# Attention products of 64 and 16 contraction rows are issued as products of all 128 rows, padded with zeros

## The chip, the cores and the metric

The kernel runs on one core of a Trainium2 chip. TensorE (PE) multiplies: a weight load puts the stationary operand into the array (one row per partition that is summed over, up to 128 rows and 128 columns), and a matmul streams the moving operand past it. VectorE (DVE), ScalarE (ACT) and GpSimd (POOL) do the elementwise work, SyncE (SP) issues the DMAs. The metric is the time of one execution in microseconds. The kernel before takes 2603.17 us, the median of three runs between 2599.4 and 2603.88 us.

## The reference, cut to what matters

Two transformer blocks run one after the other on 16 meta tokens and 512 real ones (L = 528 rows, width 1024). The first has two layers, with three kinds of attention over both blocks:

```
layer A: stick-breaking attention, 16 heads of 64: z = q k^T / 8,
         w = exp(log_sigmoid(z) + sum over later keys of log_sigmoid(-z)), o = w v
layer B: differential attention, 8 heads: o = (softmax(q1 k1^T / 8) - lam softmax(q2 k2^T / 8)) v,
         q1, q2, k1, k2 of 64 dims, v of 128
mixer:   forgetting attention, 8 heads of 64: softmax(q k^T / 8 + c_t - c_s) v,
         and a gated linear recurrence, 8 heads of 128 (chunks; the first one is the 16 meta rows)
each of A and B is followed by an MLP, the mixer by a mixture of 32 experts, 2 per token
```

All of it is float32. A float32 number x is split into a high part that the array multiplies in one pass (fp32r) and the rest x - high, and a product is high x high plus the two cross terms.

## The kernel before

TensorE's instructions stand in the order in which the program writes them; the instructions of the other engines are ordered by a scheduler from that and from priorities. Attention is a generator of steps that is interleaved with dense products (projections of the next heads, split weights taken one tile ahead by `take`, L135), by estimated times in layer A (`pace`, L230) and by fixed counts of dense steps in layer B and the mixer (`script`, L753).

Scores. The 64 dims of two heads lie on partitions 0 to 63 and 64 to 127 of one tile. `stack` (L330) makes for each head s a key operand of 128 rows: high parts in the head's own 64 rows, low parts in the other 64. `double` (L338) makes for the queries: out[s] with the high parts in all rows, and out[2] with the low parts of both heads, each in its own rows. So the scores of a region are two accumulating products, one of 128 rows (high q against high and low k) and one of 64 rows (low q against high k):

```
ops = [(zr, kz[s][:, ks], qz[s][:, a:b]), (zr, kz[s][r, ks], qz[2][r, a:b])]      # sb_qk, L475
ops = [(zr, q[s][:, qs], k[s][:, a:b]), (zr, q[2][r, qs], k[s][r, a:b])]          # scores, L787
```

In layer A a pair of heads has four units (`SB_UNITS`) with regions of 272, 144 and 16, of 400, of 272 and of 256 columns; in layer B and the mixer a pair has four query tiles with 144, 272, 400 and twice 264 key columns. A third product (identity against a mask) follows on the diagonal, and in the mixer one with the forget gates. In all there are 216 products of 64 rows: 96 in layer A (recorded at L481), 80 in layer B and 40 in the mixer (both at L793).

Values. 528 keys are four tiles of 128 and one of 16 rows: `natural` (L444) transposes v into vn[:, 0..3, :] and vn[:16, 4, :], `flip` (L822) does the same for the weights, wT. The product with v has a part of 16 rows: in layer A at L525 (`pv`), in layer B at L901 (512 columns, first of five parts), in the mixer at L1160, and in the recurrence at L1260 (kn[:16, 3, :] against vn[:16, 4, :]). These operands are plain float32, for which a matmul stands in the trace as two records. Where two heads share a bank (L525, L1160), their outputs take 64 columns of the array each.

POOL multiplies the weights of layer B by the norm's gains (L132) and does one multiplication of each rotation (L689). It works its instructions off in order.

Of the kernel before, what the change touches and what calls it, by code (L numbers as in the profile page):

```python
# [7 lines left out]
F32 = mybir.dt.float32  # L8
# [10 lines left out]
NM = 16  # L19
S = 512  # L20
# [9 lines left out]
class Net:  # L30
# [43 lines left out]
    # ---- weights: loaded some tiles ahead, split one tile ahead of their use  # L74
# [60 lines left out]
    def take(self):  # L135
        """the next weights (hi, lo)"""
        nc = self.nc
        while len(self.splitq) < 2 and self.rawq and not self.rawq[0][1]:
            raw, _ = self.rawq.pop(0)
            kt = raw.shape[1]  # L140
            hi = self.wsp.tile([128, KT, 128], F32R, name="whi")[:, :kt, :]
            lo = self.wsp.tile([128, KT, 128], F32R, name="wlo")[:, :kt, :]
            with self.tc.high_priority(offset=self.AHEAD_W):
                nc.scalar.activation(hi, raw, AF.Copy)  # L144
                nc.vector.tensor_sub(lo, raw, hi)  # L145
            self.splitq.append((hi, lo))
# [11 lines left out]
    # ---- products  # L158
# [5 lines left out]
    def product(self, w, act, a, b, ps=None, ks=None):  # L164
        """act: list of (hi, lo) of [128, n]; ks: those of its rows to take, of all"""
# [11 lines left out]
    def opening(self, act, halves, banks):  # L177
        """the products of the next weights, begun before act's last rows and the norm's sums are there"""
# [19 lines left out]
    def accumulate(self, act, halves, after=None, off=0):  # L198
        """h += act @ W tile by tile; after(t) when h[t] has its sum; act's columns begin at off"""
# [65 lines left out]
    # ---- normalisation: g * h is multiplied, the reciprocal norms come in with the products  # L265
# [4 lines left out]
    def norm_tile(self, t, ht, gains, sl=slice(0, L)):  # L270
        """ht: h[t]; its squares into the sum; g*h split in two parts for each (g, pair, columns) of gains"""
# [28 lines left out]
    def rsqrt(self, out, ps, n, t=None):  # L300
        """out = -2 (ps + eps)^-0.5, the activation tables' result refined once"""
# [73 lines left out]
    # ---- stick-breaking attention  # L375

    def sb_setup(self):
# [7 lines left out]
        self.kz, self.qz = [], []  # L385
        for i in range(2):
            self.kz.append([c.tile([128, 640], F32R, name="sbk%d%d" % (s, i)) for s in range(2)])
            self.qz.append([c.tile([128, L], F32R, name="sbq%d%d" % (s, i)) for s in range(3)])
# [3 lines left out]
    def room(self, p):  # L392
        """two heads' operands are kept"""
        while self.used < p - 1:
            yield True

    def sb_dense(self, act, o):
        ap, u = self.ap, self.UNIT
        for p in range(8):
# [4 lines left out]
            if p == 0:  # L404
                # the norm comes after the first products
# [28 lines left out]
    def banks3(self, which):  # L434
        """gives the next of some banks' tiles at each call"""
# [6 lines left out]

    def natural(self, vf, banks, cuts):
        """vf: [128, L]; its columns transposed, 4 tiles of 128 and 16 more; cuts: where each begins"""  # L444
        nc = self.nc
        vn = self.ap.tile([128, 5, 128], F32, name="vn")
# [9 lines left out]
    # regions of a unit: (key tile, first query, last query, column)  # L456
# [7 lines left out]
    def sb_qk(self, p, u):  # L464
# [3 lines left out]
        for s in range(2):  # L468
            z = self.zp.tile([128, 512], F32, name="z")
            zs.append(z)  # L470
            for g, (i, a, b, c) in enumerate(self.SB_UNITS[u]):
# [4 lines left out]
                r = slice(s * 64, s * 64 + 64)  # L476
                ops = [(zr, kz[s][:, ks], qz[s][:, a:b]), (zr, kz[s][r, ks], qz[2][r, a:b])]
# [29 lines left out]
    def sb_sum(self, dst, d0, src, s0, n):  # L507
        """the softplus sums of the later keys join those of a tile, for the tiles before it"""
# [5 lines left out]
    def sb_attn(self, o_pairs):  # L514
# [4 lines left out]
        def pv(p, u, ws):  # L519
            for i, a, b, c in self.SB_UNITS[u]:  # L520
                rows = 16 if i == 4 else 128
# [9 lines left out]
        for n, (p, u) in enumerate(units):  # L531
# [37 lines left out]
            else:  # L569
                # columns of the unit, of those with later keys, and of the later keys' sums  # L570
# [28 lines left out]
    def open_h(self, src, cols, side="right"):  # L599
        """h comes back; cols: its columns in use"""  # L600
# [39 lines left out]
    # ---- differential attention  # L640

    def df_setup(self):
# [23 lines left out]
        nc.scalar.activation(lam, lam, AF.Exp)  # L666
        self.nlam = c.tile([128, 1], F32, name="nlam")
# [10 lines left out]
    def head_norm(self, x, sq, c0, g):  # L678
        """x: [128, n] of two heads' 64 dims, normalised and rotated; c0: position of column 0"""
# [14 lines left out]
    def df_dense(self, hg, o, part):  # L694
        ap, count, due = self.ap, 0, []

        def units(*x, parts=2):
            """a dense product by steps; what is due after some of them"""
# [7 lines left out]
        for p in range(9):  # L706
            yield from self.room(p - 1)
            if p < 8:
# [3 lines left out]
                q = [ap.tile([128, S], F32R, name="dfq%d" % i, bufs=3) for i in range(3)]  # L712
# [40 lines left out]
    def script(attn, dense, drain=True):  # L753
        """as many steps of dense as attn yields, or one where it waits for dense"""
# [13 lines left out]
    def partial(self, o, part, halves, off, n):  # L768
        """the first n heads' part of the product with the output weights, into part or added to h"""
# [13 lines left out]
    def scores(self, zr, q, k, t, s, a, b, extra=None):  # L783
        """zr = q k^T of query tile t and keys a to b, causal mask on its last 128 keys"""
        nc = self.nc
        qs, r = slice(128 * t, 128 * t + 128), slice(s * 64, s * 64 + 64)
        ops = [(zr, q[s][:, qs], k[s][:, a:b]), (zr, q[2][r, qs], k[s][r, a:b])]  # L787
# [7 lines left out]
    def softmax(self, q, k, t, extra=None):  # L795
        """exponentials of query tile t's scores in two heads, and [128, 4]: -maxima, sums"""
# [26 lines left out]
    def flip(self, w, t, wT, other=False):  # L823
        """w: [128 queries, keys] of query tile t -> columns of wT (keys in partitions)"""
# [12 lines left out]
    def df_attn(self, o_pairs):  # L837
# [17 lines left out]
        def step(p, t):  # L855
            """scores of query tile t of head p"""
# [11 lines left out]
        for p in range(8):  # L868
            n = self.PAT if p < 6 else self.PAT6 if p < 7 else self.PAT7
            wT = ap.tile([128, 5, S], F32, name="wT")  # L870
# [28 lines left out]
            for i, j in enumerate((4, 0, 1, 2, 3)):  # L899
                rows = NM if j == 4 else 128  # L900
                nc.tensor.matmul(o[:, 128 * (j % 4):], vn[:rows, j, :], wT[:rows, j, 128 * (j % 4):], start=(i == 0),  # L901
# [18 lines left out]
    def layer_b(self):  # L920
# [17 lines left out]
        # h by rows of tokens for the second block's end  # L938
# [18 lines left out]
    # ---- second block: forgetting attention and the gated linear recurrence  # L957

    def mx_setup(self):
# [27 lines left out]
        nc.vector.tensor_scalar(self.lb[:, 2, :], self.lb[:, 1, :], -1.0, None, op0=ALU.mult)  # L987
        self.cq = c.tile([128, S], F32, name="cq")
# [4 lines left out]
    def log_sigmoid(self, out, x, t):  # L993
        """out = min(x, 0) - log(1 + exp(-|x|)); t: scratch"""
# [12 lines left out]
    def forget(self, hg):  # L1007
        """cumulative log forget gates of the 8 heads, split, as rows of a product's two operands"""
# [18 lines left out]
    def mx_dense(self, oa):  # L1027
# [6 lines left out]
        for p in range(5):  # L1034
            yield from self.room(p)
            if p < 4:
                qf = self.xtile(S)
                yield from units(self.evac(qf, NM, 0.125), REAL)
                fq = [self.ap.tile([128, S], F32R, name="faq%d" % i, bufs=2) for i in range(3)]
# [40 lines left out]
    def gated(self, i, x):  # L1080
        """a gate times a tile of the projection of x"""
# [12 lines left out]
    def fa_attn(self, oa):  # L1094
# [34 lines left out]
        for p in range(4):  # L1129
            n = self.PATF if p < 3 else self.PATF3  # L1130
            wT = [ap.tile([128, 5, S], F32, name="wT%d" % s) for s in range(2)]
# [25 lines left out]
            for i, j in enumerate((4, 0, 1, 2, 3)):  # L1157
                for s in range(2):
                    rows_ = NM if j == 4 else 128
                    nc.tensor.matmul(o[s * 64:s * 64 + 64, 128 * (j % 4):], vn[:rows_, j, s * 64:s * 64 + 64],  # L1160
                                     wT[s][:rows_, j, 128 * (j % 4):], start=(i == 0), stop=(i == 4),
# [34 lines left out]
    def hg_attn(self, oh):  # L1196
# [5 lines left out]
        finish = tail = None  # L1202
        for h in range(8):
# [24 lines left out]
            # decayed keys  # L1228
# [23 lines left out]
            kn = ap.tile([128, 4, 128], F32, name="kn")  # L1252
# [7 lines left out]
            nc.tensor.matmul(ps[:, :128], kn[:NM, 3, :], vn[:NM, 4, :], start=True, stop=False, skip_group_check=True)  # L1260
# [58 lines left out]
    def mixer(self):  # L1319
# [19 lines left out]
        # y = gates * projections, by tiles  # L1339
# [107 lines left out]
        # the first pairs' tokens, those of the last tile after the others  # L1447
# [23 lines left out]
    # ---- mixture of experts  # L1471
# [4 lines left out]
    def unit(self):  # L1476
        """a buffer for 128 rows of an expert's weights"""
# [35 lines left out]
    def block_weights(self):  # L1513
        """those of the expert of the first block in xi"""
# [10 lines left out]
    def first_max(self, x, m, c, idx, iota):  # L1525
        """m: maximum of each row, idx: its first place - BIG"""
# [21 lines left out]
    def select(self, R, t):  # L1548
        """the experts of the tokens in tile t and their gates"""
# [21 lines left out]
    def route(self, ts):  # L1571
        """keys of the two experts of the tokens in tiles ts: 1024 * expert + place among the expert's tokens"""
# [10 lines left out]
    def weigh(self):  # L1583
        """gates of each token's two experts"""
# [527 lines left out]
```

## Time and profile before

| | |
|---|---|
| median of three runs | 2603.17 us (2599.4 to 2603.88) |
| profiled execution: first to last instruction | 2596.9 us |
| between the two | 6.3 us, outside the first and the last instruction or between executions |
| PE matmuls busy | 2542.0 us, 98% |
| weight loads busy | 2002.4 us, 77% |
| DVE, ACT, POOL busy | 1488.5, 1157.6, 86.5 us |
| mean granted clock of TensorE | 0.987 |

The profile has one time for the profiled execution, its span. A matmul's record is longer than its turn, since matmuls are pipelined: the turn is read from start to start. A weight load (PEld) runs beside the matmul before it, so an idle stretch ahead of a weight load that ends with "issue", and not with another engine, is time in which TensorE itself held the load back. The stages by time: layer A's attention 35 to 330 us, its MLP to 745, layer B's attention 745 to 1040, its MLP to 1440, forgetting attention 1450 to 1605, the recurrence 1605 to 1860, gates and output products to 2000, the experts to the end.

### The profile page before, as it was taken

How to read it: one execution, taken by the hardware profiler on the slowest of the kernel's cores; microseconds unless marked ns; L12 is line 12 of the kernel's file. 1: busy time of each engine (PE TensorE's matmuls, PEld its weight loads, DVE VectorE, ACT ScalarE, POOL GpSimd, SP SyncE). 2: the span in 40 equal slices, each digit the busy share in tenths (PEclk: the TensorE clock that was granted, in tenths of full speed). 3: DMA queues.
4: the chain of work that ended last, by engine and by line, in shares of the span. 5: the costliest groups of instructions: out<-in, count | busy, mean ns of one | idle time of the engine just before them, and what ended most of it. 6: DMA issues, size and time to landing. Idle time of an engine off the chain costs nothing. (4 is left out here: it accounts for less than half of the span.)

```text
span 2596.9 us, 38798 instructions
## 1 busy us (share of the span) xinstructions
PE 2542.0 (98%) x15048; PEld 2002.4 (77%) x15048; DVE 1488.5 (57%) x2797; ACT 1157.6 (45%) x2181; POOL 86.5 (3%) x61
## 2 busy tenths in 40 slices
PE   8999999999989999999999999999999999999997
PEld 7888899999977777788887888999888744445442
DVE  6555563443578986633444656988754544444435
ACT  6666652332456776423323555656653222111112
POOL 0000000000032220000000000000000000000000
PEclk9999999999989999999999999999999999999998
DMA  3111132222321111423323211122234599978995
GB/s 116 45 46 37 33 102 90 90 90 90 111 88 49 49 37 37 137 91 97 96 91 114 81 49 58 58 66 66 70 121 166 220 393 407 409 307 327 409 408 215
DMA packets 110139, 361.67 MB, mean 139 GB/s; under 512 B 13440, under 2 KB 17792, under 8 KB 109952
## 3 DMA queue, kind: packets, MB, share of 16 engines
q1 hardware_dynamic: 109376, 357.05, 38.5%
q8 instruction: 120, 1.97, 0.3%
q10 hardware_dynamic: 576, 2.10, 0.2%
q14 instruction: 67, 0.55, 0.1%
HBM read 352.75 MB, written 6.36 MB: 138 GB/s over the span
## 5 line engine op out<-in xcount | busy, mean ns | idle before, releaser
L172 PE MATMUL dn<-hg_hi,whi 128*128 128x264 f32 (+1 forms) x2096 | 678.0, 323 | 9.3 <-ACT hg_hi L293 6.8
L173 PE MATMUL dn<-hg_lo,whi 128*128 128x264 f32 (+1 forms) x2096 | 664.5, 317 | 2.1 <-DVE hg_lo L294 2.0
L174 PE MATMUL dn<-hg_hi,wlo 128*128 128x264 f32 (+1 forms) x2096 | 665.0, 317 | 0.0
L144 ACT ACTIVATE whi<-wraw 128x1024 fp32r<-128x1024 f32 (+1 forms) x285 | 284.8, 999 | 616.3 <-PE dn L173 541.2
L172 PEld LDWEIGHTS dn<-hg_hi,whi 128*128 128x128 f32 x2096 | 398.6, 190 | 39.2 <-ACT hg_hi L293 6.8
L173 PEld LDWEIGHTS dn<-hg_lo,whi 128*128 128x128 f32 x2096 | 398.3, 190 | 31.2 <-DVE hg_lo L294 4.3
L174 PEld LDWEIGHTS dn<-hg_hi,wlo 128*128 128x128 f32 x2096 | 398.3, 190 | 24.8
L145 DVE TENSOR_TENSOR wlo<-wraw,whi 128x1024 fp32r<-128x1024 f32 (+1 forms) x285 | 335.7, 1178 | 94.6 <-ACT whi L144 93.1
L172 PE MATMUL dn<-rhi,whi 128*128 128x264 f32 (+1 forms) x768 | 247.0, 322 | 2.1 <-DVE h L202 1.7
L174 PE MATMUL dn<-rhi,wlo 128*128 128x264 f32 (+1 forms) x768 | 246.8, 321 | 0.0
L173 PE MATMUL dn<-rlo,whi 128*128 128x264 f32 (+1 forms) x768 | 246.7, 321 | 0.0
L202 DVE TENSOR_TENSOR h<-h,dn 128x264 f32<-128x264 f32 (+1 forms) x120 | 61.7, 514 | 199.6 <-PE dn L174 199.4
L172 PEld LDWEIGHTS dn<-rhi,whi 128*128 128x128 f32 x768 | 144.4, 188 | 14.8 <-DVE h L202 2.9
L173 PEld LDWEIGHTS dn<-rlo,whi 128*128 128x128 f32 x768 | 144.5, 188 | 11.4
L174 PEld LDWEIGHTS dn<-rhi,wlo 128*128 128x128 f32 x768 | 144.5, 188 | 11.0
L1740 PE MATMUL pa<-ew,X 128*64 128x512 f32 (+1 forms) x470 | 130.7, 595 | 1.9 <-DVE H L1745 1.9
L1740 PE MATMUL pu<-ew,X 128*64 128x512 f32 (+1 forms) x470 | 130.6, 594 | 0.1
L356 DVE SCALAR_TENSOR_TENSOR relu<-dn,rstd 128x264 f32<-128x264 f32 (+1 forms) x93 | 48.2, 519 | 130.4 <-PE dn L174 130.3
L999 DVE SCALAR_TENSOR_TENSOR H<-pa,PTq 128x512 f32<-128x512 f32 x17 | 11.7, 691 | 187.1 <-ACT PTq L998 173.6
L1768 PE MATMUL py<-ew,HT 128*64 128x512 f32 (+1 forms) x472 | 112.4, 595 | 0.7 <-ACT HT L1762 0.7
L1783 DVE TENSOR_TENSOR acc<-acc,g 128x512 f32<-128x512 f32 x136 | 86.0, 679 | 35.3 <-PE g L1782 35.3
L996 ACT ACTIVATE PTq<-pa 128x512 f32<-128x512 f32 x17 | 10.2, 597 | 197.5 <-PE pa L1740 197.5
(533 smaller groups left out, 4396.8 us busy)
## 6 DMA issues: line engine op xcount, KB each, us to landing
ew<-e_in SPq DMA_DIRECT2D x228, 512.0 KB, 10.1
ew<-e_out SPq DMA_DIRECT2D x109, 512.0 KB, 10.1
wraw<-mlp_in SPq DMA_DIRECT2D x64, 512.0 KB, 3.5
wraw<-mlp_out SPq DMA_DIRECT2D x64, 512.0 KB, 3.5
wraw<-w SPq DMA_DIRECT2D x60, 512.0 KB, 3.5
wraw<-e_in SPq DMA_DIRECT2D x28, 512.0 KB, 10.1
wraw<-a_qkv SPq DMA_DIRECT2D x24, 512.0 KB, 3.5
wraw<-kv SPq DMA_DIRECT2D x16, 512.0 KB, 3.4
```

The source lines that it names most:

```text
L144: nc.scalar.activation(hi, raw, AF.Copy)
L145: nc.vector.tensor_sub(lo, raw, hi)
L172: nc.tensor.matmul(ps, whi[:, k, :], hi[:, a:b], start=(k == 0), stop=False)
L173: nc.tensor.matmul(ps, whi[:, k, :], lo[:, a:b], start=False, stop=False)
L174: nc.tensor.matmul(ps, wlo[:, k, :], hi[:, a:b], start=False, stop=(k == len(act) - 1))
L202: self.nc.vector.tensor_add(self.h[:, t, a:b], self.h[:, t, a:b], ps)
L356: nc.vector.scalar_tensor_tensor(x, ps, 0.0, self.rstd[:, a:b], op0=ALU.max, op1=ALU.mult)
L996: nc.scalar.activation(t, x, AF.Abs)
L999: nc.vector.scalar_tensor_tensor(out, x, 0.0, t, op0=ALU.min, op1=ALU.subtract)
L1740: nc.tensor.matmul(ps[r], X[i][:, k, :], win[i][k][:, c:c + 512], start=(k == 0), stop=(k == KT - 1), skip_group_check=True)
L1768: nc.tensor.matmul(ys[c][r], HT[:, k, r], wout[i][k][:, c * 512:c * 512 + 512], start=(k == 0), stop=(k == 3), skip_group_check=True)
L1783: nc.vector.tensor_add(self.acc[:, t, cs], self.acc[:, t, cs], po)
```

## The change

Both kinds of small product get all 128 rows, with zeros in the rows that did not belong to them.

- Low query parts: instead of one tile out[2] for both heads, each head has its own tile out[2 + s], with the low parts in its 64 rows and zeros in the other 64. The zeros are written once for each stage by the new `lows` on POOL (2, 3 and 2 pairs of tiles), and the tiles are used in turn. The other operand is the key tile with all its rows (kz[s] or k[s]); its other 64 rows meet zeros.
- Meta rows: vn, wT and kn are allocated once for each stage, and their last slot is filled with zeros in all 128 rows by the new `meta_rows` (POOL); the transposes go on writing 16 of its rows. The products take the whole slot.

The numbers of products, loads, columns, activations and DMAs are the same. Comments are taken out as well, which moves line numbers (L481 becomes L499, L793 becomes L812, L132 stays).

```diff
+    def lows(self, pool, name, n, sets):
+        out = []
+        for i in range(sets):
+            pair = [pool.tile([128, n], F32R, name="%s%d%d" % (name, i, s)) for s in range(2)]
+            for s in range(2):
+                self.nc.gpsimd.memset(pair[s][self.ROWS[1 - s]].bitcast(F32), 0.0)
+            out.append(pair)
+        return out
...
-            self.nc.vector.tensor_sub(out[2][r], x[r], out[i][r])
+            self.nc.vector.tensor_sub(out[2 + i][r], x[r], out[i][r])
...
-        self.kz, self.qz = [], []
+        self.meta_rows(c, 0)
+        self.kz, self.qz, ql = [], [], self.lows(c, "sbl", L, 2)
...
+    def meta_rows(self, pool, wts):
+        self.vn = pool.tile([128, 5, 128], F32, name="vn")
+        self.wT = [pool.tile([128, 5, S], F32, name="wT%d" % i) for i in range(wts)]
+        for x in [self.vn] + self.wT:
+            self.nc.gpsimd.memset(x[:, 4, :], 0.0)
...
-                ops = [(zr, kz[s][:, ks], qz[s][:, a:b]), (zr, kz[s][r, ks], qz[2][r, a:b])]
+                ops = [(zr, kz[s][:, ks], qz[s][:, a:b]), (zr, kz[s][:, ks], qz[2 + s][:, a:b])]
...
-                            vn[:rows, i, s * 64:s * 64 + 64], ws[s][:rows, c + qa - a:c + qb - a],
+                            vn[:, i, s * 64:s * 64 + 64], ws[s][:, c + qa - a:c + qb - a],
...
+        self.ql = self.lows(c, "dfl", S, 3)
+        self.meta_rows(c, 1)
...
-        ops = [(zr, q[s][:, qs], k[s][:, a:b]), (zr, q[2][r, qs], k[s][r, a:b])]
+        ops = [(zr, q[s][:, qs], k[s][:, a:b]), (zr, q[2 + s][:, qs], k[s][:, a:b])]
...
-                nc.tensor.matmul(o[:, 128 * (j % 4):], vn[:rows, j, :], wT[:rows, j, 128 * (j % 4):], start=(i == 0),
+                nc.tensor.matmul(o[:, 128 * (j % 4):], vn[:, j, :], wT[:, j, 128 * (j % 4):], start=(i == 0),
...
+        self.ql = self.lows(c, "fal", S, 2)
+        self.meta_rows(c, 2)
...
-            nc.tensor.matmul(ps[:, :128], kn[:NM, 3, :], vn[:NM, 4, :], start=True, stop=False, skip_group_check=True)
+            nc.tensor.matmul(ps[:, :128], kn[:, 3, :], vn[:, 4, :], start=True, stop=False, skip_group_check=True)
```

On PE, ACT, DVE and SP every instruction keeps its place. TensorE's first scores of layer A, before (sbq_204 is the tile of both heads' low query parts, sbk_200 the keys, maskk the mask):

```order
L481 MATMUL z<-sbq_202,sbk_200 128x272
L481 MATMUL z<-sbq_204,sbk_200 128x272
L481 MATMUL z<-maskk,identr 128x128
L481 MATMUL z<-sbq_202,sbk_200 128x144
L481 MATMUL z<-sbq_204,sbk_200 128x144
```

And now:

```order
L499 MATMUL z<-sbq_212,sbk_210 128x272
L499 MATMUL z<-sbl_202,sbk_210 128x272
L499 MATMUL z<-maskk,identr 128x128
L499 MATMUL z<-sbq_212,sbk_210 128x144
L499 MATMUL z<-sbl_202,sbk_210 128x144
```

Nothing moved; the second product reads sbl, the head's own low parts, and has 128 rows where it had 64 (these rows name the output's 128 partitions, not the rows that are summed over).

POOL's queue gets 23 fills with zeros. Where layer B's attention begins it had, before (wraw are weights times gains, hsq a rotation):

```order
L390 MEMSET sbk_208 128x112
L132 TENSOR_TENSOR wraw<-wraw,gains 128x1024 x7
L689 TENSOR_TENSOR hsq<-hsq,rope 128x528
L689 TENSOR_TENSOR hsq<-hsq,rope 128x512
L132 TENSOR_TENSOR wraw<-wraw,gains 128x1024 x2
```

And now:

```order
L132 TENSOR_TENSOR wraw<-wraw,gains 128x1024 x4
L343 MEMSET dfl_8320 64x512
L343 MEMSET dfl_8321 64x512
L343 MEMSET dfl_8324 64x512
L343 MEMSET dfl_8325 64x512
L343 MEMSET dfl_8328 64x512
L343 MEMSET dfl_8329 64x512
L460 MEMSET vn 128x128
L460 MEMSET wT_8333 128x512
L132 TENSOR_TENSOR wraw<-wraw,gains 128x1024 x3
L708 TENSOR_TENSOR hsq<-hsq,rope 128x528
L708 TENSOR_TENSOR hsq<-hsq,rope 128x512
```

Eight fills stand between the fourth and the fifth weight. In the same way seven fills (fal, vn, two wT) stand ahead of those of cq and ck, the operands with the forget gates, where the mixer begins; four sbl and one vn at the start of the program, and vn and kn ahead of the recurrence.

## Rows read from the trace of the kernel before

**Rows 1.** The page, part 1: busy time and share of the span.

```profile
PE 2542.0 (98%) x15048; PEld 2002.4 (77%) x15048; DVE 1488.5 (57%) x2797; ACT 1157.6 (45%) x2181; POOL 86.5 (3%) x61
```

**Rows 2.** Attention stretches: length; PE, PEld, DVE, ACT, POOL busy; clock; DMA share, GB/s.

```profile
35.00:330.00 295.00, 294.64 (x2074) 256.57 (x2073) 164.30 (x366) 198.51 (x464) 0.00 (x0) 0.97 0.13 42
765.00:1040.00 275.00, 269.60 (x1419) 206.09 (x1419) 227.04 (x410) 193.33 (x426) 55.17 (x30) 0.96 0.14 43
1450.00:1605.00 155.00, 155.00 (x1017) 128.56 (x1016) 83.51 (x168) 86.17 (x184) 0.00 (x0) 1.00 0.17 55
```

**Rows 3.** Weight loads of 64 rows by shape: count, busy and mean, idle before.

```profile
L481 PEld LDWEIGHTS z<-sbq,sbk 64*128 64x128 f32 x96 | 17.6, 183 | 11.4 <-issue 3.8
L793 PEld LDWEIGHTS z<-k,dfq 64*128 64x128 f32 x80 | 15.0, 188 | 12.1 <-issue 5.2
```

**Rows 4.** Timeline, layer A, a unit of 400 columns: start, length, engine, line.

```profile
117.55 0.29 PE L174 MATMUL dn<-hg_hi,wlo 128*128 128x264 f32 x1
117.56 0.19 PEld L481 LDWEIGHTS z<-sbq,sbk 128*128 128x128 f32 x1
117.68 0.72 PE L481 MATMUL z<-sbq,sbk 128*128 128x400 f32 x2
...
117.95 0.18 PEld L481 LDWEIGHTS z<-sbq,sbk 64*128 64x128 f32 x1 [0.21 <-issue]
...
118.33 0.19 PEld L481 LDWEIGHTS z<-maskk,identr 128*128 128x128 f32 x1 [0.19 <-issue]
...
119.45 0.20 PEld L525 LDWEIGHTS o<-sbw,vn 128*64 128x64 f32 x4
```

**Rows 5.** Timeline of PE: two products of 400 columns and 128 rows.

```profile
94.51 0.35 PE L501 MATMUL z<-spl,trir 128*128 128x400 f32 x1
94.69 0.29 PE L505 MATMUL z<-sph,onesr 128*128 128x272 f32 x1
```

**Rows 6.** Timeline of PE: first unit of a pair, 18 products, and what follows.

```profile
107.78 0.60 PE L481 MATMUL z<-sbq,sbk 128*128 128x272 f32 x2
...
111.58 0.49 PE L525 MATMUL o<-sbw,vn 128*64 128x272 f32 x2
```

**Rows 7.** Timeline of PE, layer B: last query tile of a head, and what follows.

```profile
816.18 1.23 PE L793 MATMUL z<-k,dfq 128*128 128x264 f32 x4
...
818.89 0.34 PE L172 MATMUL dn<-hg_hi,whi 128*128 128x264 f32 x1
```

**Rows 8.** Timeline of PE, recurrence: the product of 16 rows and its neighbours.

```profile
1641.08 0.39 PE L174 MATMUL dn<-hg_hi,wlo 128*128 128x512 f32 x1
1641.39 0.48 PE L1260 MATMUL g<-vn,kn 16*128 16x128 f32 x2
1641.81 0.94 PE L1262 MATMUL g<-vn,kn 128*128 128x128 f32 x6
1642.50 0.48 PE L172 MATMUL dn<-hg_hi,whi 128*128 128x512 f32 x1
```

**Rows 9.** Busy time summed and averaged over four heads, 803.0 to 938.0 us.

```profile
sum 135.00, PE 132.94 PEld 103.36 DVE 124.92 ACT 98.88 POOL 36.71; mean PE 33.23 PEld 25.84 DVE 31.23 ACT 24.72 POOL 9.18
```

**Rows 10.** Who PE waited for in layer B's attention: total, times, longest.

```profile
PE dn L684 <- DVE xf L209: 3.1, 6, 0.5
```

**Rows 11.** Layer A, columns as Rows 2: a first unit, and right behind it.

```profile
108.50:111.90 3.40, 3.40 (x20) 2.59 (x19) 1.83 (x2) 2.90 (x6) 0.00 (x0) 0.99 0.21 42
111.90:115.30 3.40, 3.40 (x17) 2.85 (x14) 1.43 (x3) 2.89 (x8) 0.00 (x0) 0.51 0.31 122
```

**Rows 12.** Timelines of POOL, PE and ACT where the fills come in.

```profile
735.10 1.90 POOL L132 TENSOR_TENSOR wraw<-wraw,gains 128x1024 f32<-128x1024 f32 x1 [4.83 <-DMA wraw<-kv]
1333.22 0.54 POOL L991 MEMSET ck<- 128x528 f32 x1
...
1427.83 0.60 PE L942 MATMUL dn<-ident,h 128*128 128x128 f32 x4
...
1443.29 0.64 ACT L1022 ACTIVATE ck<-x 8x528 fp32r<-8x528 f32 x1 [2.10 <-DVE x L1020]
```

More of the change, by code (lines that the diff above doesn't have):

```diff
@@ L384, in sb_setup @@
         nc.vector.memset(self.onesr.bitcast(F32), -1.0)
-        self.kz, self.qz = [], []
+        self.meta_rows(c, 0)
+        self.kz, self.qz, ql = [], [], self.lows(c, "sbl", L, 2)
         for i in range(2):
             self.kz.append([c.tile([128, 640], F32R, name="sbk%d%d" % (s, i)) for s in range(2)])
-            self.qz.append([c.tile([128, L], F32R, name="sbq%d%d" % (s, i)) for s in range(3)])
+            self.qz.append([c.tile([128, L], F32R, name="sbq%d%d" % (s, i)) for s in range(2)] + ql[i])
             for k in self.kz[i]:
@@ L441, in banks3 @@
         return bank
+    def meta_rows(self, pool, wts):
[3 more added lines that the diff above has]
+            self.nc.gpsimd.memset(x[:, 4, :], 0.0)
     def natural(self, vf, banks, cuts):
         nc = self.nc
-        vn = self.ap.tile([128, 5, 128], F32, name="vn")
+        vn = self.vn
         ps = banks()
@@ L475, in sb_qk @@
                 m = min(128, b - a)
-                r = slice(s * 64, s * 64 + 64)
-                ops = [(zr, kz[s][:, ks], qz[s][:, a:b]), (zr, kz[s][r, ks], qz[2][r, a:b])]
+                ops = [(zr, kz[s][:, ks], qz[s][:, a:b]), (zr, kz[s][:, ks], qz[2 + s][:, a:b])]
                 if diag:
@@ L520, in pv @@
             for i, a, b, c in self.SB_UNITS[u]:
-                rows = 16 if i == 4 else 128
                 for qa, qb in ([(128, 256), (256, 528)] if i == 1 else [(a, b)]):
@@ L711, in df_dense @@
                 k = [ap.tile([128, L], F32R, name="k%d" % i, bufs=3) for i in range(2)]
-                q = [ap.tile([128, S], F32R, name="dfq%d" % i, bufs=3) for i in range(3)]
+                q = [ap.tile([128, S], F32R, name="dfq%d" % i, bufs=3) for i in range(2)] + self.ql[p % 3]
                 def keys(kf=kf, k=k):
@@ L785, in scores @@
         nc = self.nc
-        qs, r = slice(128 * t, 128 * t + 128), slice(s * 64, s * 64 + 64)
-        ops = [(zr, q[s][:, qs], k[s][:, a:b]), (zr, q[2][r, qs], k[s][r, a:b])]
+        qs = slice(128 * t, 128 * t + 128)
+        ops = [(zr, q[s][:, qs], k[s][:, a:b]), (zr, q[2 + s][:, qs], k[s][:, a:b])]
         if extra:
@@ L869, in df_attn @@
             n = self.PAT if p < 6 else self.PAT6 if p < 7 else self.PAT7
-            wT = ap.tile([128, 5, S], F32, name="wT")
+            wT = self.wT[0]
             yield n[0]
@@ L899, in df_attn @@
             for i, j in enumerate((4, 0, 1, 2, 3)):
-                rows = NM if j == 4 else 128
-                nc.tensor.matmul(o[:, 128 * (j % 4):], vn[:rows, j, :], wT[:rows, j, 128 * (j % 4):], start=(i == 0),
+                nc.tensor.matmul(o[:, 128 * (j % 4):], vn[:, j, :], wT[:, j, 128 * (j % 4):], start=(i == 0),
                                  stop=(i == 4), skip_group_check=True)
@@ L1038, in mx_dense @@
                 yield from units(self.evac(qf, NM, 0.125), REAL)
-                fq = [self.ap.tile([128, S], F32R, name="faq%d" % i, bufs=2) for i in range(3)]
+                fq = [self.ap.tile([128, S], F32R, name="faq%d" % i, bufs=2) for i in range(2)] + self.ql[p % 2]
                 self.double(qf, fq)
@@ L1130, in fa_attn @@
             n = self.PATF if p < 3 else self.PATF3
-            wT = [ap.tile([128, 5, S], F32, name="wT%d" % s) for s in range(2)]
+            wT = self.wT
             yield n[0]
@@ L1158, in fa_attn @@
                 for s in range(2):
-                    rows_ = NM if j == 4 else 128
-                    nc.tensor.matmul(o[s * 64:s * 64 + 64, 128 * (j % 4):], vn[:rows_, j, s * 64:s * 64 + 64],
-                                     wT[s][:rows_, j, 128 * (j % 4):], start=(i == 0), stop=(i == 4),
+                    nc.tensor.matmul(o[s * 64:s * 64 + 64, 128 * (j % 4):], vn[:, j, s * 64:s * 64 + 64],
+                                     wT[s][:, j, 128 * (j % 4):], start=(i == 0), stop=(i == 4),
                                      skip_group_check=True)
@@ L1202, in hg_attn @@
         finish = tail = None
+        self.meta_rows(ap, 0)
+        kn = ap.tile([128, 4, 128], F32, name="kn")
+        nc.gpsimd.memset(kn[:, 3, :], 0.0)
         for h in range(8):
@@ L1251, in hg_attn @@
             nc.tensor.transpose(ps[:NM, 384:512], kd[:, :NM], self.ident)
-            kn = ap.tile([128, 4, 128], F32, name="kn")
             nc.scalar.activation(kn[:, :3, :], ps[:, :384].rearrange("p (a b) -> p a b", a=3), AF.Copy)
```

## The prediction, as it was put on record

> **What bounds the kernel now.** I read the busy times first, then the waits of TensorE by stage, then the timeline of single products. The reader is to see in the first that TensorE's matmuls are busy for 98% of the span [rows 1], and in the second that this holds in each attention stretch: 294.64 of 295 us, 269.60 of 275 and 155 of 155, with DVE and ACT below it [rows 2]. So TensorE is the bound, and time taken out of its stream moves the end, until another engine's work is late.
>
> A busy TensorE is not a TensorE that streams columns. The weight loads of 64 rows have idle time ahead of them that mostly no engine ended ("issue" ended part of it), 11.4 us in layer A and 12.1 us in layer B [rows 3]. [...] The load of the first scores product begins at 117.56, together with the matmul ahead of it (117.55), so it is hidden under that matmul, and its own matmul follows after 0.13 us, the turn of 264 columns. [...]
>
> [...]
>
> **The change part by part, on TensorE.** One run in full: the unit of 400 columns has six products, 400, 400 and 128 columns for each of two heads, and takes from 117.68 to 119.45, 1.77 us [rows 4]. Without edges it is four times 0.18 (from the pair of 400) and once 0.11, and the last mask, behind which a change of columns stays, some 0.16: 0.99 us. The difference is 0.78 us for four edges, 0.2 us an edge. For 128 columns or fewer an edge costs less, because such products stand 0.11 us apart whatever their width (six in 0.69 us [rows 8]): the first unit, 18 products, takes 3.80 us [rows 6], and steady it is four of 272 at 0.13 (the turn of 264 columns [rows 4]) and fourteen at 0.11, 2.06 us; it loses 1.74 us for twelve edges. The last query tile in layer B (ten products) takes 2.71 us [rows 7] and steady 8 x 0.13 + 2 x 0.11 = 1.26: 1.45 us for eight edges, 0.18 each. So:
>
> - Layer A, a pair of heads: 1.74 + 0.78 + 0.78 (256 columns) + 0.6 (272, of whose four edges the last is a change of columns) = 3.9 us, times 8 pairs = 31 us.
> - Layer B, a head: 0.55 (144 columns, four edges at 0.14, near the first unit's mean of 1.74/12) + 0.8 + 0.8 + 1.45 = 3.6 us, times 8 = 29 us. Mixer, four pairs with the same widths: 14.4 us.
> - Products of 16 rows. In the recurrence the two records take 0.42 us where six of the same width take 0.69, so 0.19 too much; the product ahead has 0.31 for 512 columns, some 0.1 too much [rows 8]: 0.3 us, times 8 = 2.4. In layer B the same edges stand at the first of five parts: 0.3, times 8 = 2.4. In the mixer and layer A one side is a change of columns that stays, or 16 columns only: 0.15 x 4 + 0.1 x 8 = 1.4. Together 6 us.
>
> On TensorE alone this is 31 + 29 + 14.4 + 6 = 80 us.
>
> **The clock.** The mean granted clock is 0.97 over 295 us in layer A and 0.96 over 275 us in layer B [rows 2], so 9 and 11 us are lost there, in stretches at 1.2 GHz. In the one shown, the clock is 0.51 from 111.9 to 115.3, and TensorE's 3.4 us before it were the end of a first unit, with 20 matmul records [rows 11], where dense products at 0.13 us [rows 4] would make 26. The other four in layer A stand behind such units too, and three in layer B behind the 272-column tile and the 16-row product. With the edges gone the same columns come in just over half the time. I take 7 of layer A's 9 us as coming back; bounds are 0 and 9, and 0 and 5 for the three in layer B (3.4 us each, half of it lost; the rest stands at that layer's start, where TensorE waits). I count layer B's at nothing, since another engine decides there.
>
> **What is late next.** In layer A, ACT has 198.51 and DVE 164.30 us of work [rows 2] for the 257 us that would remain; I take 2 us as lost to single waits, bounds 0 and 15 (half). In the mixer both are below 87 of 155 us; nothing is lost. In layer B it is different. Over four heads of 33.75 us each, DVE is busy for 31.23 us a head [rows 9]: it can give up 2.5 us a head at most, 20 us for eight heads, while TensorE's saving is 3.6 + 0.3 = 3.9 us a head. Six waits of TensorE on DVE's evacuation of keys are there already [rows 10]. The first and the last head have more room, and DVE will not run without a gap: I take 17 of the 31 us. Bounds: 0, if every gap of DVE is a latency that stays, and 36, all of it and the clock.
>
> **The fills.** POOL gets 23 fills. A fill of 128x528 takes 0.54 us [rows 12], so none of them is longer. Layer B's eight, 4.3 us, stand ahead of the weight that is multiplied at 735.10, and POOL sits idle for 4.83 us before it; their tiles lie where layer A's attention had its own. The mixer's seven, 3.8 us, stand ahead of cq and ck; some of their tiles are read by the MLP until its last product, behind which the transposes stand at 1427.83, and ACT first writes ck at 1443.29 [rows 12], so 11 us of cover are left. Those at the start have 35 us. I cost them at nothing; without cover they would be 4.3 and 3.8 us once.
>
> **The sum.** Layer A 31 + 1 + 7 - 2 = 37; layer B 17; mixer 14.4 + 0.6 = 15; recurrence 2.4: 71 us. The span would be 2597 - 71 = 2526 us, and the time, with the 6.3 us between the span and the median, 2603 - 71 = 2532 us.
>
> **The rivals.**
> - The whole of it arrives. DVE in layer B is busy partly with operations that POOL's multiplications stretch, and a shorter stretch need not keep all of it; then layer B gives 36 us and layer A 41: 94 us, 2509 us. For it: TensorE hardly waits today. Against it: DVE's 31.23 of 33.75 us.
> - Latencies eat more. ACT and DVE work in chains (maximum, exponential, reciprocal, scaling), and TensorE, arriving earlier, waits at fixed places of its order: layer A gives 16 and no clock, layer B 5, mixer 15, recurrence 2: 38 us, 2565 us. For it: the waits on DVE exist [rows 10]. Against it: in the mixer and layer A there is next to no idle time of TensorE to begin with [rows 2].
> - The change doesn't do what it says: the idle time is not the change of rows but that of operands, and stays; then 2603 us. Against it: the mask product, 128 rows, with operands of its own, has the idle time only because 64 rows stand ahead of it [rows 4], and the product of 16 rows has it at its edges too [rows 8].
> [...]
>
> **How the numbers follow.** Forecast (60 to 85 us gained, 2518 to 2543) 0.62; all of it (2500 to 2518) 0.13; latencies (2543 to 2585) 0.21; no change 0.025; slower 0.015. A measurement of this kernel tells 0.2%, 5 us, from no change. So faster 0.96, same 0.025, slower 0.015. The range takes the forecast, half of the first rival and the near half of the second: 2512 to 2556.
>
> **What would show it.** Right: the 64-row and 16-row forms are gone; no "issue" gap stands ahead of the loads of scores; the unit of 400 columns takes 1.0 us instead of 1.77, the first unit 2.1 instead of 3.80; the mixer's attention shrinks from 155 to 140 us; layer A's granted clock is near 1.00; a head of layer B takes 31 to 32 us, with DVE at 97% and waits of TensorE on DVE that have grown. Wrong: gaps of 0.2 us still ahead of the padded loads (then the change of rows is not their cause); layer B's heads near 29.8 us (then DVE was no limit); or stretches at 1.2 GHz that stay where they are.

## The result and the profile after

The median is 2530.47 us (2528.38 to 2530.76, four runs), the one before 2603.53 us (four runs): a ratio of 0.9722, with a 95% interval of 0.9709 to 0.9736. The profiled execution's span went from 2596.9 to 2529.0 us, 67.9 us. The kernel before was timed again beside the experiments, with medians of 2599.42 and 2598.95 us (seven runs each), so some 4 of the 73 us between the medians may be the scatter of the kernel before.

Part 1 of the page, after [rows 1]:

```profile
PE 2458.7 (97%) x15048; PEld 1981.4 (78%) x15048; DVE 1480.9 (59%) x2797; ACT 1150.9 (46%) x2181; POOL 98.3 (4%) x83
```

The stretches between the same instructions as in [rows 2]: layer A, layer B, forgetting attention, and the recurrence. The columns are length; PE, PEld, DVE, ACT, POOL busy; clock; DMA share, GB/s.

```profile
35.00:293.80 258.80, 256.98 (x2077) 240.75 (x2076) 164.77 (x366) 193.06 (x464) 0.00 (x0) 0.99 0.16 48
728.50:991.40 262.90, 240.92 (x1420) 202.71 (x1420) 223.01 (x411) 193.15 (x427) 58.29 (x30) 0.96 0.15 45
1400.40:1539.90 139.50, 139.50 (x1018) 125.02 (x1017) 82.40 (x168) 86.09 (x184) 0.41 (x2) 1.00 0.20 61
1539.90:1791.80 251.90, 251.90 (x1716) 229.74 (x1715) 225.98 (x468) 152.20 (x273) 0.00 (x0) 1.00 0.19 61
```

Layer A lost 36.2 us, the mixer 15.5, the recurrence 3.1 (of the 255 between 1605 and 1860 us). Layer B lost 12.1, or 13.5 between the first and the last of its instructions (295.9 to 282.4, from 709.0 to 991.4 us). Only in layer B has TensorE become idle for long (in layer A for 1.8 us): 240.92 of 262.90 us are busy, where it was 269.60 of 275.

The timeline of a unit of 400 columns, after [rows 4]:

```profile
107.97 0.29 PE L174 MATMUL dn<-hg_hi,wlo 128*128 128x264 f32 x1
107.98 0.19 PEld L499 LDWEIGHTS z<-sbq,sbk 128*128 128x128 f32 x1
108.10 0.34 PE L499 MATMUL z<-sbq,sbk 128*128 128x400 f32 x1
108.10 0.19 PEld L499 LDWEIGHTS z<-sbl,sbk 128*128 128x128 f32 x1
108.28 0.34 PE L499 MATMUL z<-sbl,sbk 128*128 128x400 f32 x1
...
109.08 0.44 PE L542 MATMUL o<-sbw,vn 128*64 128x256 f32 x2
```

The load of the low parts (sbl) now begins at 108.10 with the matmul ahead of it, and its own matmul follows 0.18 us later. The unit takes 0.98 us instead of 1.77. The first unit [rows 6] and layer B's last query tile [rows 7], each from its first product to what follows:

```profile
101.49 0.29 PE L499 MATMUL z<-sbq,sbk 128*128 128x272 f32 x1
...
103.55 0.45 PE L542 MATMUL o<-sbw,vn 128*64 128x272 f32 x2
```

```profile
774.42 0.28 PE L812 MATMUL z<-k,dfq 128*128 128x264 f32 x1
...
775.57 0.33 PE L172 MATMUL dn<-hg_hi,whi 128*128 128x264 f32 x1
```

They take 2.06 and 1.15 us instead of 3.80 and 2.71. The loads that answer to [rows 3] have no idle time left ahead of them (count, busy, mean ns, idle):

```profile
L499 PEld LDWEIGHTS z<-sbl,sbk 128*128 128x128 f32 x96 | 18.2, 190 | 0.0
L812 PEld LDWEIGHTS z<-k,dfl 128*128 128x128 f32 x80 | 15.7, 196 | 0.5 <-issue 0.2
```

The recurrence's product of meta rows [rows 8]:

```profile
1575.51 0.40 PE L174 MATMUL dn<-hg_hi,wlo 128*128 128x512 f32 x1
1575.74 0.38 PE L1281 MATMUL g<-vn,kn 128*128 128x128 f32 x2
1575.96 0.83 PE L1283 MATMUL g<-vn,kn 128*128 128x128 f32 x6
1576.55 0.48 PE L172 MATMUL dn<-hg_hi,whi 128*128 128x512 f32 x1
```

The product ahead takes 0.23 us instead of 0.31, the meta rows 0.22 instead of 0.42, the six behind them 0.59 instead of 0.69: 0.38 us less.

Layer B's four middle heads [rows 9] gained nothing: 135.0 us before and 135.5 after. All four together, before and after (columns as in the first table of stretches), and whom TensorE waited for in them after (total, times, longest; [rows 10] has the waits before):

```profile
803.30:938.30 135.00, 132.94 (x736) 103.47 (x734) 124.92 (x212) 99.17 (x219) 37.01 (x20) 0.97 0.14 45
762.70:898.20 135.50, 122.14 (x735) 104.41 (x734) 123.84 (x213) 99.21 (x219) 40.06 (x20) 0.95 0.15 47
```

```profile
PE dn L703 <- DVE xf L209: 8.4, 4, 2.1
PE dn L928 <- DVE xf L209: 4.2, 4, 1.3
```

TensorE's busy time fell by 10.8 us and its idle time grew by 11.3, from 2.1 to 13.4. DVE's work is what it was, 123.84 us against 124.92. One wait of 2.1 us stands in each head, and behind each of these four TensorE's granted clock is 0.50 or 0.51 for 3.4 us (from 791.7, 825.8, 859.9 and 894.1 us). One of them, timeline of PE:

```profile
825.74 1.21 PE L703 MATMUL dn<-hsq,blk 128*128 128x264 f32 x2 [2.09 <-DVE xf L209]
...
827.41 0.42 PE L172 MATMUL dn<-hg_hi,whi 128*128 128x264 f32 x1
827.63 0.42 PE L173 MATMUL dn<-hg_lo,whi 128*128 128x264 f32 x1
```

Products of 264 columns stand 0.22 us apart there instead of 0.12: 1.2 columns a ns, which the prediction and the expectations call 1.2 GHz. In layer A one such stretch is left of the five before (a clock of 0.50 or 0.51 for 3.4 us from 43.6, 111.9, 149.4, 221.1 and 292.8 us; [rows 11] has the second), and ahead of it TensorE was busy for only 1.89 of 3.40 us (same columns):

```profile
44.20:47.60 3.40, 1.89 (x18) 1.65 (x16) 2.88 (x8) 3.35 (x8) 0.00 (x0) 1.00 0.00 0
47.60:51.00 3.40, 3.40 (x17) 3.40 (x17) 3.23 (x11) 2.65 (x9) 0.00 (x0) 0.50 0.00 0
```

So the questions were two: is it the change of rows that cost the time, and what holds layer B's middle heads at 135 us?

### The profile page after: what moved, and what is told of

Its sections match the earlier page's. It is cut to its first block, busy times and chain, and to the rows that moved or that the text cites. A ratio compares the mean times of both kernels' runs of the same rounds, so it can differ in the third digit from the quotient of the medians.

```text
span 2529.0 us, 38832 instructions
## 1 busy us (share of the span) xinstructions
PE 2458.7 (97%) x15048; PEld 1981.4 (78%) x15048; DVE 1480.9 (59%) x2797; ACT 1150.9 (46%) x2181; POOL 98.3 (4%) x83
## 5 line engine op out<-in xcount | busy, mean ns | idle before, releaser
L173 PEld LDWEIGHTS dn<-rlo,whi 128*128 128x128 f32 x768 | 144.5, 188 | 11.4
L1019 DVE SCALAR_TENSOR_TENSOR H<-pa,PTq 128x512 f32<-128x512 f32 x17 | 11.7, 691 | 187.1 <-ACT PTq L1018 173.6
## 6 DMA issues: line engine op xcount, KB each, us to landing
ew<-e_in SPq DMA_DIRECT2D x228, 512.0 KB, 10.1
ew<-e_out SPq DMA_DIRECT2D x109, 512.0 KB, 10.1
wraw<-e_in SPq DMA_DIRECT2D x28, 512.0 KB, 10.1
```

Source lines behind the costliest of these rows:

```text
L173: nc.tensor.matmul(ps, whi[:, k, :], lo[:, a:b], start=False, stop=False)
L1019: nc.vector.scalar_tensor_tensor(out, x, 0.0, t, op0=ALU.min, op1=ALU.subtract)
```

## The experiments

All times are medians of four runs of the kernel named, and the ratios are to the kernel before on the same chip. The changed kernel was not timed again beside them; since the median of the kernel before moved by some 4 us between the series, a difference from the changed kernel of that size says nothing.

**1. The change of rows alone, without padding.** The kernel before, with the products of a unit in another order: all of 128 rows of both heads, then those of 64 rows, then the masks. Operands and products are those of before.

```diff
-                ops = [(zr, kz[s][:, ks], qz[s][:, a:b]), (zr, kz[s][r, ks], qz[2][r, a:b])]
+                first.append((zr, kz[s][:, ks], qz[s][:, a:b], g == 0, False))
+                low.append((zr, kz[s][r, ks], qz[2][r, a:b], False, not diag))
...
+        for o, x, y, st, sp in first + low + last:
+            nc.tensor.matmul(o, x, y, start=st, stop=sp, skip_group_check=True)
```

> The kernel before, with the scores products of a unit or query tile in another order: all products of 128 rows of both heads first, then all of 64 rows (the first head's, then the second's), then the masks. Nothing is padded and no product is added or left out. Theory (the cost sits at each change between 128 and 64 rows): the edges fall from 12 to 2, 4 to 2, 3 to 1 and 4 to 2 in layer A's four units and from 4 to 2 in each query tile (8 to 4 in the last), so 21 us come back in layer A (plus 0 to 4 of the clock), about 7 in the mixer and about 6 in layer B: 2565 to 2575 us; some 8 us less if going from one head's 64 rows to the other's costs an edge too. Rival (the cost sits at each product of 64 rows, whatever stands ahead of it): 2598 to 2605 us, nothing gained.

Measured: 2547.48 us (2544.31 to 2550.99), ratio 0.9802 (0.9785 to 0.9819). The same 216 products of 64 rows are there, and most of the cost is gone with the order. The loads of 64 rows in layer A have 4.2 us of idle time ahead of them instead of 11.4 [rows 3], and a first unit, with its six products of 64 rows, takes 1.90 us from its first product to what follows (3.80 before, 2.06 padded):

```profile
L481 PEld LDWEIGHTS z<-sbq,sbk 64*128 64x128 f32 x96 | 7.9, 184 | 4.2 <-issue 1.7
```

```profile
103.75 1.20 PE L481 MATMUL z<-sbq,sbk 128*128 128x272 f32 x12
...
105.65 0.45 PE L524 MATMUL o<-sbw,vn 128*64 128x272 f32 x2
```

So the change of rows is what costs, and not each product of 64 rows. The run gained more than expected. Its timeline of a unit of 400 columns shows one reason (x2: two instructions in one row):

```profile
110.18 0.90 PE L481 MATMUL z<-sbq,sbk 128*128 128x400 f32 x4
...
110.64 0.19 PEld L481 LDWEIGHTS z<-sbq,sbk 64*128 64x128 f32 x2 [0.19 <-issue]
...
111.02 0.30 PEld L481 LDWEIGHTS z<-maskk,identr 128*128 128x128 f32 x2 [0.19 <-issue]
```

The two loads of 64 rows, one for each head, fit into the 0.19 us of one, and the masks' load follows 0.38 us after them, as long as after a single product of 64 rows in [rows 4]. The two heads' products lie in different halves of the rows, and the pair took the 0.38 us of one. So a grouped unit has two edges instead of four, and its second product of 64 rows costs no time of its own: not all of the 52 us are edges. Padding is still 17 us better, but not in layer B's four middle heads:

```profile
769.00:900.20 131.20, 121.77 (x735) 98.26 (x734) 123.30 (x213) 98.52 (x219) 37.95 (x20) 1.00 0.15 46
```

They take 131.2 us grouped and 135.5 padded, with nearly the same busy time of TensorE and DVE. What differs is TensorE's waits (at most 1.6 us at the place where they are 2.1 us padded) and its clock, 1.00 against 0.95. Products grouped in layer B and padded elsewhere were not run.

**2. Layer B's scores back in 64 rows.** The changed kernel, with only the low parts of layer B as before.

```diff
-        ops = [(zr, q[s][:, qs], k[s][:, a:b]), (zr, q[2 + s][:, qs], k[s][:, a:b])]
+        r = slice(0, 128) if extra else slice(s * 64, s * 64 + 64)
+        ops = [(zr, q[s][:, qs], k[s][:, a:b]), (zr, q[2 + s][r, qs], k[s][r, a:b])]
```

> The changed kernel, with the low query parts of layer B alone taken in 64 rows again (the tiles with zeros and their fills stay). Theory (DVE sets the pace of layer B's middle heads): only the first and the last heads lose, some 13 us: 2541 to 2546 us, and the four heads in the middle keep their 33 to 34 us each. Rival (TensorE's stream sets the pace there as well): 80 products at 0.36 us, 29 us: about 2559 us, each head in the middle some 3.6 us longer.

Measured: 2540.99 us (2538.57 to 2542.57), ratio 0.9774 (0.9758 to 0.979). By the prediction's count the undone part is worth 29 us on TensorE; it moves the time by 10.5. The four middle heads together, and TensorE's longest wait in them:

```profile
770.00:902.60 132.60, 129.52 (x736) 102.02 (x734) 125.14 (x212) 98.37 (x219) 38.02 (x20) 1.00 0.15 46
```

```profile
PE dn L703 <- DVE xf L209: 2.1, 4, 0.5
```

With 7.4 us more of TensorE's work, these heads are 2.9 us shorter than with padding. TensorE waits at L703 for 2.1 us in all instead of 8.4, and its granted clock is 1.00 instead of 0.95. DVE's busy time is nearly the same, 125.14 us against 123.84. So TensorE's own work is not what holds the padded heads: a TensorE that runs ahead there loses its lead in waits for DVE and in the clock behind them. That DVE sets the pace is not shown by this run, in which TensorE itself is busy for 129.52 of 132.6 us; the next ones test it. What the kernel loses, it loses ahead of these heads (59.7 us instead of 53.7) and behind them (100.1 instead of 93.2).

**3. No multiplications by gains.** The changed kernel without POOL's 24 multiplications of layer B's weights (the gains are missing from the result).

```diff
-                self.nc.gpsimd.tensor_mul(raw, raw, g[:, :, None].to_broadcast([128, KT, 128]))
+                pass
```

> The changed kernel without POOL's multiplications of layer B's weights by the gains of the two norms (23 of them; the gains are left out of the result, the split weights are the raw ones). Theory 1 (POOL's multiplications stretch DVE's operations beside them, 2.0 us for one of 128x144 where one of 128x528 takes 0.76, and DVE sets the pace): DVE's work falls from 31 to some 26 us a head, a head in the middle takes about 30.5 us, layer B becomes 20 to 25 us shorter: 2505 to 2511 us. Theory 2 (DVE's own work or the chains between DVE, ACT and TensorE set the pace): 0 to 5 us shorter, 2525 to 2530 us. Theory 3 (the stretch at 1.2 GHz in each head is the cause, not DVE): DVE's durations do not change, the heads stay at 33 us or more.

Measured: 2506.64 us (2505.08 to 2509.08), ratio 0.9646 (0.963 to 0.9662). Nothing was taken from DVE, yet over the middle heads its busy time fell by 18 us, and the heads by 17.5:

```profile
sum 118.00, PE 114.72 PEld 98.52 DVE 105.86 ACT 98.93 POOL 13.11; mean PE 28.68 PEld 24.63 DVE 26.47 ACT 24.73 POOL 3.28
```

The same operation in the changed kernel and without the multiplications (count, busy, mean ns, idle):

```profile
L314 DVE SCALAR_TENSOR_TENSOR ors<-sq,ors 128x512 f32<-128x512 f32 x4 | 9.2, 2310 | 0.1
```

```profile
L314 DVE SCALAR_TENSOR_TENSOR ors<-sq,ors 128x512 f32<-128x512 f32 x4 | 2.8, 693 | 0.1
```

One of the four in the changed kernel, beside what POOL did (timelines):

```profile
783.75 1.90 POOL L132 TENSOR_TENSOR wraw<-wraw,gains 128x1024 f32<-128x1024 f32 x1 [5.61 <-DMA wraw<-b_q]
783.92 2.28 DVE L314 SCALAR_TENSOR_TENSOR ors<-sq,ors 128x512 f32<-128x512 f32 x1
```

DVE's operation begins 0.17 us after POOL's and ends 0.55 us after POOL's end (783.75 + 1.90 = 785.65): most of its 2.28 us it waits for POOL. A multiplication on POOL costs DVE 18 / 12 = 1.5 us.

**4. The gains inside the split, in small pieces.** Each weight's gains applied by ACT and DVE while they split it, in 8 operations of 128 columns each instead of one.

```diff
-                self.nc.gpsimd.tensor_mul(raw, raw, g[:, :, None].to_broadcast([128, KT, 128]))
...
+                    for k in range(KT):
+                        nc.scalar.activation(hi[:, k, :], raw[:, k, :], AF.Copy, scale=g[:, k:k + 1])
+                    for k in range(KT):
+                        nc.vector.scalar_tensor_tensor(lo[:, k, :], raw[:, k, :], g[:, k:k + 1], hi[:, k, :],
+                                                       op0=ALU.mult, op1=ALU.subtract)
```

> The changed kernel with the gains of layer B's norms multiplied in where the weights are split: eight ACT copies of 128 columns with a scale for each weight tile, and eight DVE operations (raw times gain minus high part), instead of POOL's multiplication; nothing is left out. Theory 1: DVE loses the stretching, 5 us a head, and gains some 1.5 us of small operations; ACT goes from 25 to 28 us a head; heads take about 31 us: 2508 to 2520 us. Theory 2: DVE and ACT only get more to do: 2530 to 2545 us.

Measured: 2543.07 us (2542.62 to 2550.17), ratio 0.9792 (0.9773 to 0.981): slower than the changed kernel, outside theory 1's range and inside theory 2's. The rows of the middle heads show that the edit brought a cost of its own (count, busy, mean ns, idle; then waits):

```profile
L150 ACT ACTIVATE whi<-wraw,gains 128x128 fp32r<-128x128 f32 x96 | 31.0, 393 | 0.1
L152 DVE SCALAR_TENSOR_TENSOR wlo<-wraw,gains,whi 128x128 fp32r<-128x128 f32 x96 | 28.4, 343 | 1.0 <-ACT whi L150 1.0
```

```profile
PE dn L711 <- DVE xf L217: 8.2, 4, 2.5
PE o L927 <- ACT wT L859: 7.9, 3, 2.8
```

The 96 pieces on DVE take 28.4 us where the 12 subtractions of 128x1024 took 14.6, which eats what the stretch gave back (DVE is busy for 120.24 us over the four heads), and TensorE now waits for ACT as well. With a cost of its own in it, the experiment doesn't tell the theories apart; the next three do.

**5 to 7. One gain multiplication a head; the rotation off POOL too; all multiplications on DVE.** Two thirds of POOL's multiplications go if the first gain is multiplied into the activations where they are split, and the second is divided by the first:

```diff
+        gr = c.tile([128, KT], F32, name="gr")
+        nc.vector.reciprocal(gr, self.gains[:, 2 * KT:3 * KT])
+        nc.vector.tensor_mul(self.gains[:, 3 * KT:4 * KT], self.gains[:, 3 * KT:4 * KT], gr)
...
-                        yield w["kv"][p], KT, 2
+                        yield w["kv"][p], KT
...
-                        yield w["kv"][7 + p], KT, 2
+                        yield w["kv"][7 + p], KT
...
-            self.norm_tile(t, self.h[:, t, :], [(None, self.hg, ALL)])
+            self.norm_tile(t, self.h[:, t, :], [(2, self.hg, ALL)])
```

> The changed kernel, with layer B's first gain multiplied into the activations where they are split and the second gain divided by the first, so that POOL multiplies 8 weights of layer B instead of 24 (the result is the same function). Theory 1, POOL's multiplications stretch DVE and DVE sets the pace of layer B's middle heads: without all 24 the time fell by 24 us and DVE's work by 1.5 us per multiplication (123.84 to 105.86 us over four heads, 12 multiplications), so with 16 fewer 12 to 20 us fall away: 2510 to 2519 us, middle heads 30 to 31.5 us with DVE at about 28 us each, and the stretches at 1.2 GHz behind a wait on DVE in each middle head gone. Theory 2, the 24 us came from something else that went with the gains, the waits of the weights in POOL's queue: one multiplication a head keeps that queue, 2525 to 2531 us.

Measured: 2519.55 us (2517.79 to 2521.03), ratio 0.9693 (0.9677 to 0.9709): 10.9 us below the changed kernel, half a microsecond above theory 1's bound and outside theory 2. The stretches at half the granted clock were expected to go from all four middle heads; two still have a clock of 0.95 and 0.97. The sum of the heads:

```profile
sum 126.90, PE 117.75 PEld 100.68 DVE 112.38 ACT 99.16 POOL 20.80; mean PE 29.44 PEld 25.17 DVE 28.09 ACT 24.79 POOL 5.20
```

Then the rotation:

```diff
-        nc.gpsimd.tensor_mul(sq, sq, self.rope[:, 1, c0:c0 + n])
+        nc.vector.tensor_mul(sq, sq, self.rope[:, 1, c0:c0 + n])
```

> The same, and the multiplication of each rotation goes from POOL to DVE. Theory 1: DVE takes on two operations of some 0.7 us a head and loses the stretch that is left beside the rotations (the 128x272 operation at L869, 1.57 us where 0.76 us is the price of 528 columns): about nothing, 2508 to 2520 us. Theory 2, every operation more on DVE sets the pace in full: 8 heads by 1.4 us, 11 us slower than the kernel with one gain.

Measured: 2512.63 us (2511.25 to 2514.22), ratio 0.9664 (0.9648 to 0.968), the fastest kernel here with the whole result, and in theory 1's range. DVE took on two operations a head and its work did not grow:

```profile
sum 123.90, PE 116.04 PEld 99.91 DVE 111.82 ACT 97.96 POOL 7.70; mean PE 29.01 PEld 24.98 DVE 27.95 ACT 24.49 POOL 1.93
```

What the multiplications cost on DVE (5.5 us over four heads) they had cost it from POOL. And all 24 gain multiplications on DVE, the changed kernel otherwise:

```diff
-                self.nc.gpsimd.tensor_mul(raw, raw, g[:, :, None].to_broadcast([128, KT, 128]))
+                self.nc.vector.tensor_mul(raw, raw, g[:, :, None].to_broadcast([128, KT, 128]))
```

> The changed kernel, with all 24 gain multiplications of 128x1024 on DVE instead of POOL. Theory 1, a multiplication on POOL costs DVE 1.5 us of stretch, one on DVE itself some 1.22 us (as the subtraction of 128x1024 at L145): DVE's work falls by 0.8 us a head, the time by 0 to 10 us, 2520 to 2531 us. Theory 2, POOL's multiplications cost DVE nothing: DVE's work grows by 3.6 us a head, 2545 to 2560 us.

Measured: 2533.68 us (2532.48 to 2535.55), ratio 0.9747 (0.9731 to 0.9763), between the ranges of both theories and close to the first. The sum of the middle heads, and rows of DVE in them (count, busy, mean ns, idle):

```profile
sum 136.90, PE 121.49 PEld 102.49 DVE 124.33 ACT 99.64 POOL 14.02; mean PE 30.37 PEld 25.62 DVE 31.08 ACT 24.91 POOL 3.50
```

```profile
L132 DVE TENSOR_TENSOR wraw<-wraw,gains 128x1024 f32<-128x1024 f32 x12 | 14.7, 1222 | 2.9 <-DMA wraw<-kv 2.9
L707 DVE TENSOR_TENSOR xf<-xf,rope 128x528 f32<-128x528 f32 x4 | 7.3, 1831 | 0.0
L707 DVE TENSOR_TENSOR xf<-xf,rope 128x512 f32<-128x512 f32 x4 | 6.8, 1704 | 0.0
```

Twelve multiplications take 14.7 us of DVE, and its busy time is 124.33 us against 123.84 with them on POOL. The two are so close partly by chance: the operations at L707 now run beside POOL's rotations and take 14.1 us instead of 5.6, while the one that stood beside them in the changed kernel, L869 at 272 columns, takes 1.9 us instead of 6.3. By itself a multiplication of 128x1024 cost DVE 1.2 us on DVE (1222 ns in the row above) and 1.5 us on POOL (experiment 3), so having it on POOL saved DVE nothing.

## Why the prediction was right, and where it was off

The forecast of 2532 us stands 1.5 us from the median. That it is so near is partly luck. The span was forecast at 2526 us and came out at 2529.0. The 6.3 us that were added for the time between span and median are 1.8 us in the runs after (2530.76 against 2529.0), so most of the 6.3 us was that the profiled execution of the kernel before was one of the shorter ones. In its steps:

- **The edges.** Right. An edge is a change between 128 and 64 rows in TensorE's stream. Before, the load of 64 rows began 0.27 us after the product ahead of it (117.68 and 117.95 [rows 4]), where products of 400 columns and 128 rows stand 0.18 us apart [rows 5], and the load of 128 rows behind it began another 0.38 us later. Padded, the loads stand 0.18 us apart (108.10 and 108.28). 0.99 us were worked out for the unit of 400 columns and 0.98 measured, 2.06 and 2.06 for the first unit, 1.26 and 1.15 for layer B's last tile. The unit's last mask, put at 0.16 us for the change of columns behind it, took 0.15 (108.93 to 109.08). Experiment 1 shows the cause: with products and operands unchanged, the order alone takes 52 us off, a part of it because two products of 64 rows then take the 0.38 us of one.
- **Layer A, 37 us.** Measured 36.2. The clock came back as taken: four of five stretches are gone, 0.97 became 0.99.
- **The mixer, 15, and the recurrence, 2.4.** Measured 15.5 and 3.1. The recurrence was mis-sized at the six products behind the meta rows: their 0.69 us had been taken as steady and hold an edge too (0.59 after).
- **Layer B, 17 us of TensorE's 31.** Measured 13.5, and the sum hides that the step failed in part. "It can give up 2.5 us a head at most" took DVE's gaps for time that could be given up. In the middle heads nothing was: DVE's gaps were 10.1 us over the four heads and are 11.7, and the gain is none, the lower bound. A head was to take 31 to 32 us with DVE at 97%; it takes 33.9 with DVE at 91%. The gaps are not all fixed latencies either, for they are 7.9 us in experiment 1 and 7.5 in experiment 2. Layer B's clock was counted at nothing, and it takes some 3 us more there (0.02 of 135): the stretches at a granted clock of 0.50, 3.4 us each, went from two to four. The part ahead of them (745 to 803 us before) gave 4.5 us and the part behind them (938 to 1041) 9.5. That DVE would decide was right: relieved of 18.0, 11.5 and 12.0 us over the four heads (experiments 3, 5 and 6), they are 17.5, 8.6 and 11.6 us shorter.
- **The fills.** Right: POOL has 22 instructions more (22 fills, not 23) and is busy for 11.8 us more, and no wait of TensorE on POOL appears.
- **The sum.** 71 us were forecast and 67.9 measured in the span; the medians differ by 73, and the rest may be the scatter named above. The steps' errors (layer B -3.5, layer A -0.8, the others +1.2) are within the range.

Of the rivals, the whole of it arriving named what stood in its way: DVE's operations that POOL stretches. Relieved of most of them, with the whole result, the kernel takes 2512.63 us; that this is near the rival's 2509 says little, since it is another kernel with less work on DVE. The rival of latencies named what the middle heads show, a wait of TensorE at one fixed place in each, but not its size elsewhere: layer A's idle time grew by 1.5 us. That nothing would change, or that the kernel would get slower, is refuted: the padded loads have 0.0 us (L499) and 0.5 us (L812) of idle time ahead of them, and the span fell by 67.9 us.

What stays open is why a wait of TensorE of 2.1 us is followed by a granted clock of 0.50 for 3.4 us in all four middle heads after, while in experiment 5 the waits at the same place are as long (up to 2.1 us, six of them 9.9 us in all between 700 and 1000 us), and two of the four heads keep a clock of 1.00.

## What to carry to other kernels

Look for idle time ahead of weight loads that no engine ends (here 23.5 us at the loads of 64 rows [rows 3]): where products of few rows stand among products of 128, pad them with zeros (73 us here), or at least put those of equal rows together (52 us, experiment 1). Before time is credited to TensorE, ask of the engine that is next at the limit what its busy time is made of: here an operation of 0.69 us was recorded with 2.31 because it waited for another engine, and the gaps between its operations gave nothing back. Elementwise work on POOL beside a busy DVE was not free here (1.5 us of DVE for each multiplication of 128x1024, experiment 3); folding two thirds of it into operations that were there anyway took 10.9 us off (experiment 5).

## What the runs showed of the hardware

- **POOL holds up DVE.** Beside a multiplication of 128x1024 on POOL, an operation of 128x512 at L314 took 2.31 us, and 0.69 us without (experiment 3); one of 128x144 at L869 took 2.00 us, and 0.36 us without. The one at 783.92 ended 0.55 us after POOL's multiplication had; the one at L869 that began at 792.68 ended at 794.68, 0.15 us after POOL's (792.13 to 794.53). A multiplication cost DVE 1.5 us.
- **Two products of 64 rows in different halves took the time of one** when they followed each other (experiment 1: two loads within 0.19 us, and the next load of 128 rows 0.38 us behind them, as behind one).
- **A faster TensorE lost part of its gain to its clock.** In the middle heads the granted clock fell from 0.97 to 0.95 with padding (0.02 of 135 us, some 3 us), and was 1.00 with the slower products of experiment 2 and with the grouped ones of experiment 1.
